# A two-layer decoder on one core: when the RMS norms' squares and mean columns are issued

## The chip, the cores and the metric

The kernel runs on one core of one Trainium2 chip. The metric is the device time of one execution in microseconds; the lower, the better. Engines are named as in the profile: PE is TensorE, ACT is ScalarE, DVE is VectorE, POOL is GpSimd, and SP's queue issues the loads.

## What is computed

The input x has 256 tokens of 1024 features, and every weight and activation is float32. Two layers are run, each as half a feed-forward step, an attention mixer, and half a feed-forward step:

```python
def rmsnorm(x, g):
    y = x * lax.rsqrt(jnp.mean(x * x, axis=-1, keepdims=True) + RMS_EPS)
    return y * g

def swiglu(h, w_gate, w_up, w_down):          # 1024 -> 2816 -> 1024
    return (jax.nn.silu(h @ w_gate) * (h @ w_up)) @ w_down

for layer in range(2):
    h = h + 0.5 * swiglu(rmsnorm(h, ffn1_norm[layer]), ...)
    hn = rmsnorm(h, mix_norm[layer])
    h = h + (mixer_a(hn, a_w_qkv, a_w_o) if layer == 0 else mixer_b(hn, b_w_q, b_w_o, *shared))
    h = h + 0.5 * swiglu(rmsnorm(h, ffn2_norm[layer]), ...)
    if layer == 0:
        shared = shared_kv(h, kv_norm, kv_w)  # keys and values for mixer_b
return rmsnorm(h, final_norm)
```

Both mixers are attention with 16 heads of 64 and rotary on 16 of the 64 features. What matters here is the norm: the factor `rsqrt(mean(x*x) + eps)` belongs to a token, so it can be applied after the products with the weights, to their result.

## The kernel before

**Precision.** Every float32 factor is split in two on the chip: a high part (`wh`, `xh`), a rounding copy on ACT, and a low part (`wl`, `xl`), the difference taken on DVE. Each product is three: high by high, high by low, low by high. In `products_t` (L198) the activations' high and low parts stand side by side, so that a weight's high part takes both in one 512-wide matmul (L203), and its low part takes the activations' high part in a 256-wide one (L206). In `product` (L189), used by the mixers, three matmuls of 512 stand in a row (L192, L194, L196).

**Order.** All instructions are written in program order; a scheduler then orders each engine's queue. `queued(p)` (L145) fixes one instruction behind another on its engine where the author wishes so, without a semaphore: whatever is issued within it stands behind the instructions that `marks[p]` holds.

**The norm.** `Norm` (L219 to L260) holds what is needed of one RMS norm. `scale` multiplies the residual stream by the gain and splits it (`x_n`: ACT L98, DVE L96). `square` squares one of the eight feature blocks on ACT (`ss_n` for the first, L237, and `sq_n` for the seven others, L240) and adds it to the running sum on POOL (L241). `finish` makes the column: four small matmuls of the sum with 1/1024 (`col_n`, PE L246), the epsilon (`v_n`, DVE L248) and the power -0.5 (`c_n`, POOL L250). `spread` makes a row of the column, for results that have features on the partitions: two diagonal matrices (`diag_n`, DVE L257), four matmuls with ones (`row_n`, PE L258) and a copy out of PSUM (`r_n`, DVE L260).

**The feed-forward opening.** `ffn_blocks` (L351) walks over the 22 blocks of 128 hidden features, two at a time. The first pair of the first layer, `f10`, is special: `opening` (L172) loads its weights in slices along the features as they arrive, splits each (`wh` at L181, `wl` at L182) and multiplies at once, feature block by feature block. `first` (L805), called per slice, loads the input, scales the blocks of this slice and squares those of the slice before. The last two squares and `norm.finish()` stand behind the loop (L410 to L413), so the column's matmuls are on PE between the opening's products and those of block 2. Block 2's gate and up products (`f_g`, `f_u`, from 1 MB loads that `unit` splits at L166 and L167) follow, then `close_all`, which spreads the row and closes the blocks before: `joined` (L332) adds an accumulator's two halves (`j_f_g`, `j_f_u`: ACT L335, DVE L336), and further steps multiply by the row. Accumulators are five PSUM buffers in a ring (`accp`), so block 3's gate product `f_g3` takes the one that block 0's gate leaves. Squares and `j_` tiles share a ring of five in SBUF (`ep`).

**The mixers.** `mixer` (L722) runs its query, key and value projections through an `Agenda`: each product of the projection advances a clock by 0.68, and calls that were put down with `agenda.after(wait, ...)` are issued once the clock reaches them. The norm's remaining steps are put down at 1.5 and on, and `norm.finish` at 8.1, in mixer a for `n1` and in mixer b for `n5` (the norm of its queries; its keys' and values' norm is finished earlier). When a projection of 128 tokens is complete, `evacuate` scales it by the column out of PSUM (`rt_a`, ACT L772), the rotary follows on DVE (L635 to L638), and `turn_in` transposes it on PE (`qt_a`, L761), put down 4.4 - 1.2 t behind it for token block t. `Pieces` (L292) splits the projection weights a few units ahead (`wh` on ACT L318, `wl` on DVE L320) and loads those behind them.

Of the kernel before, what the change touches and what calls it, by code (L numbers as in the profile page):

```python
# [12 lines left out]
AF = mybir.ActivationFunctionType  # L13
# [4 lines left out]
NT = S // P  # L18
D = 1024
KD = D // P  # L20
# [46 lines left out]
def trunk(ctx: ExitStack, tc: tile.TileContext, a: dict, out: bass.AP):  # L67
# [19 lines left out]
    def flat(ap):  # L87
        return ap.rearrange("p c n -> p (c n)")
# [83 lines left out]
    def opening(wg, wu, before):  # L172


        for k, n in OPENING:
            raw = early.get(k) or rawp.tile([P, 2, n, S], F32, tag="raw", name=f"raw_0_{k}")
            wh, wl = [wp.tile([P, 2, n, S], F32R, tag=tag, name=f"{tag}_0_{k}") for tag in ("wh", "wl")]
            before(k, n)
            for i, w in list(enumerate((wg, wu)))[k in early:]:
                nc.sync.dma_start(raw[:, i], rows(w, k, n, 0, S))  # L180
            nc.scalar.activation(wh, raw, AF.Copy)  # L181
            nc.vector.tensor_sub(wl, raw, wh.bitcast(F32))  # L182
            for j in range(n):
                yield [(wh[:, i, j, :], wl[:, i, j, :]) for i in range(2)]
# [10 lines left out]
        for ac, (wh, wl) in zip(accs, ws):  # L195
            nc.tensor.matmul(ac, xl, wh, start=False, stop=last)  # L196

    def products_t(acs, wss, xs, first, last):  # L198


        for ac, ws in zip(acs, wss):
            for i, ((wh, wl), x) in enumerate(zip(ws, xs)):
                nc.tensor.matmul(ac, wh, flat(x), start=first and i == 0, stop=False)  # L203
        for ac, ws in zip(acs, wss):
            for i, ((wh, wl), x) in enumerate(zip(ws, xs)):
                nc.tensor.matmul(ac[:, :S], wl, x[:, 0, :], start=False, stop=last and i == len(ws) - 1)  # L206
# [12 lines left out]
    class Norm:  # L219
# [23 lines left out]
        def finish(self):  # L243
            ps = trt(f"col_{self.name}")
            for t in range(NT):
                nc.tensor.matmul(ps[:, t:t + 1], self.ss[:, t * P:(t + 1) * P], mean, start=True, stop=True)  # L246
            v = sp.tile([P, NT], F32, tag="var", name=f"v_{self.name}")
            nc.vector.tensor_scalar_add(v, ps[:, :NT], EPS)  # L248
            r = sp.tile([P, NT], F32, tag="rms", name=f"c_{self.name}")
            nc.gpsimd.tensor_tensor(r, v, expo.to_broadcast([P, NT]), op=ALU.pow)  # L250
            self.col = [r[:, t:t + 1] for t in range(NT)]
# [40 lines left out]
    class Pieces:  # L292
# [1 line left out]


        def __init__(self, specs):
            self.specs, self.raws, self.parts, self.rest = specs, [], [], []

        def load(self, u):
            while len(self.raws) <= min(u, len(self.specs) - 1):  # L300
# [6 lines left out]
        def split(self, i):  # L307

            end = 2 * len(self.specs)
            while len(self.parts) <= min(i, end - 1):  # L310
                m = len(self.parts)
                u, j = divmod(m, 2)
                self.load(u + 2)
                name, k, n, _ = self.specs[u]
                k //= 2
                raw = self.raws[u][:, j * k:j * k + k]
                wh, wl = [wp.tile([P, k, n], F32R, tag=tag, name=f"{tag}_{name}_{j}") for tag in ("wh", "wl")]
                nc.scalar.activation(wh, raw, AF.Copy)  # L318
                self.parts.append([(wh[:, r, :], wl[:, r, :]) for r in range(k)])
                self.rest.append(lambda wl=wl, raw=raw, wh=wh: nc.vector.tensor_sub(wl, raw, wh.bitcast(F32)))  # L320
                while len(self.rest) > (m < end - 1):
                    self.rest.pop(0)()

        def __getitem__(self, i):
            return self.get(i)
# [25 lines left out]
    def ffn_blocks(name, wg, wu, norm, first=None, beside=(), sums=None, queue=()):  # L351

        blocks, pairs, rest = [], {}, []

        def both(f, pair):
            acs = [acc(f"{name}_{n}{f}") for n in "gu"]
            cols = slice(f % 2 * P, (f % 2 + 1) * P)
            products_t(acs, [[(wh[:, cols], wl[:, cols]) for wh, wl in w] for w in pair], norm.x, True, True)  # L360
            return acs

        def close(f, gate, up):
            g = joined(gate, f"{name}_g{f}")
            nc.vector.tensor_mul(g, g, norm.row)  # L365
            nc.scalar.activation(g, g, AF.Silu)  # L366
            u = joined(up, f"{name}_u{f}")
            nc.gpsimd.tensor_tensor(u, u, norm.row, op=ALU.mult)  # L368
            pair = f // 2
            if sums is not None and pair in sums:  # L370
                if f % 2 == 0:
                    pairs[pair] = atile([P, 2, S], name=f"act2_{name}_{f}")
                prod = pairs[pair][:, f % 2]
            else:
                prod = g
            nc.vector.tensor_mul(prod, g, u)  # L376
            x = atile([P, 2, S], F32R, name=f"act_{name}_{f}")
            parts_of(x[:, 0], x[:, 1], prod)
            while rest:
                rest.pop(0)()  # L380
            if prod is not g and f % 2:
                rest.extend(quarter_sums(pairs.pop(pair), *sums[pair], f"{name}_{f}"))
            blocks.append(x)

        done = []

        def close_all():
            if done and norm.row is None:
                norm.spread()
            for args in done:  # L390
                close(*args)
            done.clear()

        for f in range(0, KF, 2):
            if f == 0 and first is not None:
                ws = opening(wg, wu, first)
            else:
                ws = zip(*[unit(f"{name}_{n}{f}", KD, S, [(None, rows(w, 0, KD, f * P, S))], behind[:2 if f == 0 else 0])
                           for n, w, behind in (("g", wg, queue[:2]), ("u", wu, queue[2:]))])
            if f == 0:  # L400
                acs = [[(trt if i and n == "u" else acc)(f"{name}_{n}{i}") for n in "gu"] for i in range(2)]
                for k, pair in enumerate(ws):
                    for i in range(2):
                        for ac, (wh, wl) in zip(acs[i], pair):
                            cols = slice(i * P, (i + 1) * P)
                            products_t([ac], [[(wh[:, cols], wl[:, cols])]], norm.x[k:k + 1], k == 0, k == KD - 1)
                    while norm.late:
                        norm.late.pop(0)()
                if first is not None:
                    for k in range(KD - 2, KD):  # L410
                        norm.square(k)
                if norm.col is None:
                    norm.finish()  # L413
                done += [(i, *acs[i]) for i in range(2)]
                continue
            pair = list(zip(*ws))
            for call in beside[f // 2 - 1:f // 2]:
                call()
            for i in (f, f + 1):
                acs = both(i, pair)  # L420
                close_all()
                done.append((i, *acs))
        close_all()
        return blocks
# [297 lines left out]
    def mixer(name, segs, plan, wo, mask, after, queue={}):  # L722
# [15 lines left out]
        specs += [(f"{name}o_{u}", 2, D, [(None, rows(wo, 2 * u, 2, 0, D))]) for u in range(KD // 2)]  # L738
        pieces = Pieces(specs)
        agenda = Agenda()  # L740
        for norm in {id(norm): norm for norm, _, _ in segs}.values():
            for i in range(len(norm.late)):
                agenda.after(1.5 + 0.5 * i, lambda norm=norm: norm.late.pop(0)())
            if norm.col is None:
                agenda.after(8.1, norm.finish)
        scores, turn, values = attention(agenda, lambda g: (qks[g], vss.get(g)), mask, name, blocks)

        def turns(p):
# [18 lines left out]
        def evacuate(i, t, r, ac, parts):  # L767
# [16 lines left out]
                    at += n  # L784
            for g in sorted(set(turned)):
                if ("q", g, t) in heads and ("k", g, t) in heads:
                    agenda.after(4.4 - 1.2 * t if i == 0 else 3.2, turn_in, g, t)

        def projections():
            for i, (norm, x, parts) in enumerate(segs):  # L790
                acs = [acc(f"{''.join(part[0] for part in parts)}_{name}{i}_{t}") for t in range(NT)]
                for k0 in range(0, KD, 4):
                    for t in range(NT):
                        for k in range(k0, k0 + 4):
                            w = pieces[4 * i + k // 2][k % 2]
                            product([acs[t]], *x[t](k), [w], k == 0, k == KD - 1)
                            yield 0.68
                        if k0 + 4 == KD:
                            evacuate(i, t, norm.col[t], acs[t], parts)

        agenda.run(projections())
        agenda.run(out_t(f"{name}o", pieces, base, blocks, after, queue))
# [2 lines left out]
    def first(k, n):  # L805
        cols = slice(GX + k * S if k else 0, GX + (k + n) * S)
        nc.sync.dma_start(both[:, cols], a["gains_xT"][:, cols])
        for i in range(k, k + n):
            n0.scale(i)
        for i in range(k - 2, k - 2 + n):  # L810
            if i >= 0:
                n0.square(i)

    n0, n1, n2 = Norm(0, "n0"), Norm(1, "n1"), Norm(2, "n2")
    n3, n5, n6 = Norm(4, "n3"), Norm(5, "n5"), Norm(6, "n6")
# [108 lines left out]
```

## Time and profile before

| | before |
|---|---|
| median of 3 runs | 980.28 us (980.27 to 980.37) |
| the profiled execution | 980.13 us |
| its span, first to last instruction | 978.4 us |
| granted TensorE clock | 0.998 |
| PE busy | 967.5 us, 99% |
| DVE busy | 813.0 us, 83% |
| ACT busy | 612.7 us, 63% |
| POOL busy | 287.0 us, 29% |
| HBM | 176 MB moved, 180 GB/s in the mean |

A row of the timeline gives the start in microseconds from the span's start, the duration, the engine, the line, the operation, what it writes from what it reads, a count where equal instructions follow each other, and in brackets the engine's idle time before it and what ended that. Buffer numbers are left out of names, so `wl_f_g` is the low part of any gate weight. A PE row's duration includes the time that a product takes to drain; how close two products follow is read from their starts.

### The profile page before, as it was taken

The page shows a single profiled execution, that of the slowest core. Times are in us where ns is not written, and L with a number is a line of the kernel's source. Part 1 is how long each engine was busy: PE and PEld are TensorE (multiplying, and loading weights), DVE is VectorE, ACT ScalarE, POOL GpSimd, SP SyncE. Part 2 cuts the span into 40 slices and gives each one's busy share as a digit, 9 for nine tenths or more (in the row PEclk, how much of TensorE's full clock was granted, in tenths as well). Part 3 has the DMA queues.
Part 4 walks back from the last instruction along what each step waited for, and adds up shares of the span by engine and source line. Part 5 has one row for each costly group of instructions (what it writes and reads, how often), then busy time and mean ns, then how long its engine had stood idle before and what let it go on. Part 6 is the DMA issues. An engine that isn't in the chain of part 4 may idle for free.

```text
span 978.4 us, 14860 instructions
## 1 busy us (share of the span) xinstructions
PE 967.5 (99%) x5391; PEld 831.9 (85%) x5391; DVE 813.0 (83%) x1383; ACT 612.7 (63%) x1131; POOL 287.0 (29%) x242
## 2 busy tenths in 40 slices
PE   8999999999999999999999999999999999999997
PEld 6888888878889888888888888888888998888886
DVE  7988899887878788889898888987787878888995
ACT  7655657567777665556576655655677756666561
POOL 3211246132332211146032121612142322112461
PEclk9999999999999999999999999999999999999999
DMA  9875536664334556546755556483734345564341
GB/s 317 259 238 187 197 133 216 219 212 157 133 98 152 180 186 189 184 153 208 256 172 173 172 177 212 169 277 114 249 131 136 116 145 172 186 202 173 130 172 43
DMA packets 126857, 176.00 MB, mean 180 GB/s; under 512 B 3392, under 2 KB 106304, under 8 KB 126784
## 3 DMA queue, kind: packets, MB, share of 16 engines
q1 hardware_dynamic: 125936, 174.01, 53.7%
q10 hardware_dynamic: 848, 1.05, 0.3%
q8 instruction: 42, 0.69, 0.3%
q14 instruction: 31, 0.25, 0.1%
HBM read 173.99 MB, written 1.05 MB: 179 GB/s over the span
## 4 chain that ended last, share of the span: by engine, by line
PE 92%; DVE 4%; ACT 2%; issue 1%; POOL 1%; DMA 0%; SPq 0%; POOLq 0%; DVEq 0%; ACTq 0%
PE f_g L203 16%; PE f_u L203 16%; PE f_u L206 8%; PE f_g L206 8%; PE dn_f_d L196 6%; PE dn_f_d L192 6%; PE dn_f_d L194 6%; PE dn_f_d_m L196 1%; PE dn_f_d_m L194 1%; PE dn_f_d_m L192 1%; PE qk_a L192 1%; PE qk_a L196 1%; PE qk_a L194 1%; DVE x_n L96 1%; PE q_b L192 1%
## 5 line engine op out<-in xcount | busy, mean ns | idle before, releaser
L368 POOL TENSOR_TENSOR j_f_u<-j_f_u,r_n 128x256 f32<-128x256 f32 x88 | 92.3, 1051 | 360.8 <-DVE j_f_u L336 338.0
L203 PE MATMUL f_g<-x_n,wh_f_g 128*128 128x512 f32 x688 | 180.5, 394 | 0.0
L203 PE MATMUL f_u<-x_n,wh_f_u 128*128 128x512 f32 x688 | 177.2, 390 | 0.0
L203 PEld LDWEIGHTS f_u<-x_n,wh_f_u 128*128 128x128 f32 x688 | 129.2, 188 | 27.3
L203 PEld LDWEIGHTS f_g<-x_n,wh_f_g 128*128 128x128 f32 x688 | 124.0, 189 | 22.7
L167 DVE TENSOR_TENSOR wl_f_u<-raw_f_u,wh_f_u 128x1024 fp32r<-128x1024 f32 x86 | 113.1, 1316 | 1.1 <-ACT wh_f_u L166 1.0
L167 DVE TENSOR_TENSOR wl_f_g<-raw_f_g,wh_f_g 128x1024 fp32r<-128x1024 f32 x86 | 104.3, 1230 | 2.8 <-ACT wh_f_g L166 2.8
L206 PE MATMUL f_u<-x_n,wl_f_u 128*128 128x256 f32 x688 | 103.3, 283 | 0.0
L206 PE MATMUL f_g<-x_n,wl_f_g 128*128 128x256 f32 x688 | 102.7, 282 | 0.0
L206 PEld LDWEIGHTS f_g<-x_n,wl_f_g 128*128 128x128 f32 x688 | 96.4, 190 | 6.3
L166 ACT ACTIVATE wh_f_u<-raw_f_u 128x1024 fp32r<-128x1024 f32 x86 | 88.0, 1049 | 12.0 <-PE f_g L203 7.5
L166 ACT ACTIVATE wh_f_g<-raw_f_g 128x1024 fp32r<-128x1024 f32 x86 | 89.6, 1049 | 4.7 <-PE f_g L203 2.8
L206 PEld LDWEIGHTS f_u<-x_n,wl_f_u 128*128 128x128 f32 x688 | 91.6, 192 | 0.0
L366 ACT ACTIVATE j_f_g<-j_f_g 128x256 f32<-128x256 f32 x88 | 36.7, 417 | 87.2 <-DVE j_f_g L365 86.9
L241 POOL TENSOR_TENSOR ss_n<-ss_n,sq_n 128x256 f32<-128x256 f32 x42 | 38.4, 913 | 148.8 <-ACT sq_n L240 146.8
L98 ACT ACTIVATE act_f<-j_f_g 128x256 fp32r<-128x256 f32 x58 | 23.9, 418 | 56.4 <-DVE j_f_g L376 56.4
L376 DVE TENSOR_TENSOR j_f_g<-j_f_g,j_f_u 128x256 f32<-128x256 f32 x58 | 27.9, 487 | 30.1 <-POOL j_f_u L368 30.1
L484 POOL TENSOR_TENSOR sum_f_d_6b<-sum_f_d_6ac,raw_f_d 128x512 f32<-128x512 f32 x4 | 45.5, 11371 | 17.6 <-DVE sum_f_d_6ac L483 13.2
L336 DVE TENSOR_TENSOR j_f_g<-f_g,j_f_g 128x256 f32<-128x256 f32 x88 | 36.6, 416 | 11.9 <-ACT j_f_g L335 11.9
L677 POOL TENSOR_SCALAR sm_b<-sm_b,ls_b 128x128 f32<-128x128 f32 (+1 forms) x32 | 28.5, 907 | 55.7 <-DVE ls_b L675 29.6
L335 ACT ACTIVATE j_f_u<-f_u 128x256 f32<-128x256 f32 x88 | 33.0, 375 | 15.0 <-PE row_n L258 14.0
L365 DVE TENSOR_TENSOR j_f_g<-j_f_g,r_n 128x256 f32<-128x256 f32 x88 | 41.4, 474 | 0.7
(565 smaller groups left out, 2369.3 us busy)
## 6 DMA issues: line engine op xcount, KB each, us to landing
raw_f_d<-in_ffn_w_down_dram SPq DMA_DIRECT2D x44, 1024.0 KB, 4.9
raw_f_g<-in_ffn_w_gate_dram SPq DMA_DIRECT2D x43, 1024.0 KB, 5.2
raw_f_u<-in_ffn_w_up_dram SPq DMA_DIRECT2D x43, 1024.0 KB, 5.2
raw_qka<-in_a_w_qkv_dram SPq DMA_DIRECT2D x16, 512.0 KB, 4.7
raw_va<-in_a_w_qkv_dram SPq DMA_DIRECT2D x4, 1024.0 KB, 5.4
raw_ao<-in_a_w_o_dram SPq DMA_DIRECT2D x4, 1024.0 KB, 4.9
raw_kvb<-in_kv_w_dram SPq DMA_DIRECT2D x8, 512.0 KB, 4.7
raw_qb<-in_b_w_q_dram SPq DMA_DIRECT2D x4, 1024.0 KB, 5.9
```

Of the source, the lines that this page charges most:

```text
L166: nc.scalar.activation(wh, r, AF.Copy)
L167: nc.vector.tensor_sub(wl, r, wh.bitcast(F32))
L192: nc.tensor.matmul(ac, xh, wh, start=first, stop=False)
L194: nc.tensor.matmul(ac, xh, wl, start=False, stop=False)
L196: nc.tensor.matmul(ac, xl, wh, start=False, stop=last)
L203: nc.tensor.matmul(ac, wh, flat(x), start=first and i == 0, stop=False)
L206: nc.tensor.matmul(ac[:, :S], wl, x[:, 0, :], start=False, stop=last and i == len(ws) - 1)
L241: nc.gpsimd.tensor_tensor(self.ss, self.ss, sq, op=ALU.add)
L365: nc.vector.tensor_mul(g, g, norm.row)
L366: nc.scalar.activation(g, g, AF.Silu)
L368: nc.gpsimd.tensor_tensor(u, u, norm.row, op=ALU.mult)
L484: nc.gpsimd.tensor_tensor(b[:, 0], ac[:, 0], raw[:, 3], op=ALU.add)
```

## The change

Three things move; the operations and their numbers stay as they are.

1. In the opening of `f10` all eight squares are issued behind the loop, and on ACT behind the last split of the opening's weights (`marks["opening"]`). Their adds on POOL follow them.
2. `norm.finish` of this norm is no longer called behind the opening but inside block 2's `products_t`, behind the eight wide products of its gate. The instructions on each engine stand as follows by this: on PE the column comes behind those eight and ahead of the eight wide up products; on DVE `v_n` stands behind the four `wl` subtractions of block 2, the two `diag_n`, one subtraction of block 4 and `r_n` follow, and the first `j_f_g` comes behind `r_n`, where it stood ahead of the row before. Other feed-forward steps finish their norm as before.
3. In the mixers the column is put down at 8.7 for the first norm (mixer a) and at 14.0 for the other (mixer b); the subtractions of `Pieces` that come later are queued behind `v_n` on DVE; the evacuation of a projection goes through the agenda too, 0.6 later while the column is missing; and `turn_in` comes 4.4 - 0.8 t behind. The attention's steps, which are put down from there, come about one product later against PE's queue. The loads of the rotary table, the masks and the final gain each go one step earlier among the weight loads.

```diff
         def opening / for k, n in OPENING:
-            nc.scalar.activation(wh, raw, AF.Copy)
+            marks["opening"] = [nc.scalar.activation(wh, raw, AF.Copy)]
             nc.vector.tensor_sub(wl, raw, wh.bitcast(F32))
...
-    def products_t(acs, wss, xs, first, last):
+    def products_t(acs, wss, xs, first, last, between=None):
         for ac, ws in zip(acs, wss):
             for i, ((wh, wl), x) in enumerate(zip(ws, xs)):
                 nc.tensor.matmul(ac, wh, flat(x), start=first and i == 0, stop=False)
+            if between is not None:
+                between()
+                between = None
...
-            nc.vector.tensor_scalar_add(v, ps[:, :NT], EPS)
+            marks[self.name] = [nc.vector.tensor_scalar_add(v, ps[:, :NT], EPS)]
...
-            self.specs, self.raws, self.parts, self.rest = specs, [], [], []
+            self.specs, self.raws, self.parts, self.rest, self.behind = specs, [], [], [], None
...
-                while len(self.rest) > (m < end - 1):
-                    self.rest.pop(0)()
+                with queued(self.behind):
+                    while len(self.rest) > (m < end - 1):
+                        self.rest.pop(0)()
...
-            products_t(acs, [[...] for w in pair], norm.x, True, True)
+            products_t(acs, [[...] for w in pair], norm.x, True, True,
+                       norm.finish if norm.col is None else None)
...
                 if first is not None:
-                    for k in range(KD - 2, KD):
-                        norm.square(k)
-                if norm.col is None:
+                    with queued("opening"):
+                        for k in range(KD):
+                            norm.square(k)
+                elif norm.col is None:
                     norm.finish()
...
+        def column(norm):
+            norm.finish()
+            pieces.behind = norm.name
+
             if norm.col is None:
-                agenda.after(8.1, norm.finish)
+                agenda.after(8.7 if norm is segs[0][0] else 14.0, column, norm)
...
-                    agenda.after(4.4 - 1.2 * t if i == 0 else 3.2, turn_in, g, t)
+                    agenda.after(4.4 - 0.8 * t if i == 0 else 3.2, turn_in, g, t)
...
                         if k0 + 4 == KD:
-                            evacuate(i, t, norm.col[t], acs[t], parts)
+                            agenda.after(0.6 if norm.col is None else 0.0,
+                                         lambda t=t, i=i, norm=norm, ac=acs[t], parts=parts:
+                                         evacuate(i, t, norm.col[t], ac, parts))
...
         def first:
         for i in range(k, k + n):
             n0.scale(i)
-        for i in range(k - 2, k - 2 + n):
-            if i >= 0:
-                n0.square(i)
```

More of the change, by code (lines that the diff above doesn't have):

```diff
@@ L359, in both @@
             cols = slice(f % 2 * P, (f % 2 + 1) * P)
-            products_t(acs, [[(wh[:, cols], wl[:, cols]) for wh, wl in w] for w in pair], norm.x, True, True)
+            products_t(acs, [[(wh[:, cols], wl[:, cols]) for wh, wl in w] for w in pair], norm.x, True, True,
+                       norm.finish if norm.col is None else None)
             return acs
```

## The prediction

> **What bounds the kernel now.** I read the page's engine table first, then the chain that ended last, then TensorE's list of waits, and only then the timeline around each wait.
>
> ```profile
> span 978.4 us, 14860 instructions
> PE 967.5 (99%) x5391; PEld 831.9 (85%) x5391; DVE 813.0 (83%) x1383; ACT 612.7 (63%) x1131; POOL 287.0 (29%) x242
> PE f_g L206 <- DVE wl L182: 0.8, 1, 0.8
> PE f_g L203 <- ACT wh L181: 0.8, 2, 0.5
> PE col_n L246 <- POOL ss_n L241: 0.6, 1, 0.6
> PE qt_a L761 <- ACT wh_qka L318: 0.2, 1, 0.2
> PE qt_a L761 <- DVE rt_a L638: 0.2, 1, 0.2
> ```
>
> TensorE is busy for 967.5 of 978.4 us, so a change that leaves its products alone can only win back gaps between them. The last five rows are all of its listed waits but the warm-up's, and the change aims at each of them. All are under a microsecond: 2.6 us in sum, with further tenths around them that "busy" hides, because a product that waits for a late operand inside its pipeline is shown as running. I therefore read starts, not idle columns: a 512-wide product is followed by the next start 0.23 us later, a 256-wide one 0.12.
>
> **Opening, TensorE's side.** These are TensorE's rows, then ScalarE's, VectorE's and GpSimd's.
>
> ```profile
> 9.63 0.50 PE L203 MATMUL f_g<-x_n,wh 128*128 128x512 f32 x1 [0.46 <-ACT wh L181]
> 16.08 0.39 PE L203 MATMUL f_g<-x_n,wh 128*128 128x512 f32 x1
> 17.28 0.38 PE L206 MATMUL f_g<-x_n,wl 128*128 128x256 f32 x1 [0.81 <-DVE wl L182]
> 19.93 0.50 PE L246 MATMUL col_n<-mean,ss_n 128*128 128x1 f32 x4
> 20.29 2.10 PE L203 MATMUL f_g<-x_n,wh_f_g 128*128 128x512 f32 x8
> 22.23 1.98 PE L203 MATMUL f_u<-x_n,wh_f_u 128*128 128x512 f32 x8
> 25.96 0.60 PE L258 MATMUL row_n<-diag_n,ones 128*128 128x128 f32 x4
> 26.32 0.94 PE L203 MATMUL f_g<-x_n,wh_f_g 128*128 128x512 f32 x3
> ```
> ```profile
> 12.64 0.71 ACT L240 ACTIVATE sq_n<-gains_hT 128x256 f32<-128x256 f32 x2
> 13.26 1.04 ACT L181 ACTIVATE wh<-raw 128x1024 fp32r<-128x1024 f32 x1
> 15.66 2.01 ACT L166 ACTIVATE wh_f_g<-raw_f_g 128x1024 fp32r<-128x1024 f32 x2 [0.75 <-DMA raw_f_g<-in_ffn_w_gate_dram]
> 18.67 2.01 ACT L166 ACTIVATE wh_f_u<-raw_f_u 128x1024 fp32r<-128x1024 f32 x2 [1.01 <-DMA raw_f_u<-in_ffn_w_up_dram]
> ```
> ```profile
> 9.61 1.23 DVE L182 TENSOR_TENSOR wl<-raw,wh 128x1024 fp32r<-128x1024 f32 x1 [0.90 <-ACT wh L181]
> 15.47 1.75 DVE L182 TENSOR_TENSOR wl<-raw,wh 128x1024 fp32r<-128x1024 f32 x1
> 17.15 2.89 DVE L167 TENSOR_TENSOR wl_f_g<-raw_f_g,wh_f_g 128x1024 fp32r<-128x1024 f32 x2
> 20.47 0.16 DVE L248 TENSOR_SCALAR v_n<-col_n 128x2 f32<-128x2 f32 x1 [0.43 <-PE col_n L246]
> 21.46 0.48 DVE L257 TENSOR_SCALAR diag_n<-ident,c_n 128x128 f32<-128x128 f32 x2 [0.83 <-POOL c_n L250]
> 21.86 2.35 DVE L167 TENSOR_TENSOR wl_f_u<-raw_f_u,wh_f_u 128x1024 fp32r<-128x1024 f32 x2
> 24.13 0.42 DVE L336 TENSOR_TENSOR j_f_g<-f_g,j_f_g 128x256 f32<-128x256 f32 x1
> ```
> ```profile
> 8.71 0.74 POOL L241 TENSOR_TENSOR ss_n<-ss_n,sq_n 128x256 f32<-128x256 f32 x1 [7.42 <-ACT sq_n L240]
> 13.18 4.64 POOL L241 TENSOR_TENSOR ss_n<-ss_n,sq_n 128x256 f32<-128x256 f32 x4 [0.47 <-ACT sq_n L240]
> L368 POOL TENSOR_TENSOR j_f_u<-j_f_u,r_n 128x256 f32<-128x256 f32 x88 | 92.3, 1051 | 360.8 <-DVE j_f_u L336 338.0
> ```
>
> Before, six of the eight squares stand on ScalarE between the casts (`wh`), at 0.31 us each, and their adds on GpSimd run beside VectorE's subtractions. The cost is on both: the last `wl` takes 1.75 us where one with GpSimd idle took 1.23, and it starts late. Behind the last `wh` the squares cost the opening nothing. The loads still bind: two 1 MB weight loads ended ScalarE's waits at 15.66 and 18.67, 3.0 us apart, so the load ahead of them landed near 12.65, and `wh` can go from 13.26 to 12.65, no earlier. It ends at 13.69, its `wl` near 15.0 instead of 17.22. The step of 1.20 us from 16.08 to 17.28 then shrinks to 0.23 (0.97 won); the 0.46 before 9.63 goes too, since `wh` there stands behind two squares (0.61); two smaller late operands make about 0.45. Together 1.9 us: the opening's products end near 18.05 instead of 19.93.
>
> **Opening, what is late next.** The column needs all seven adds. The squares now run from 13.7; the first add from 14.4. An add alone took 0.74, four beside VectorE took 4.64, or 1.16 each. So the sum is complete between 14.4 + 7 x 0.74 = 19.6 and 14.4 + 7 x 1.16 = 22.5. VectorE is idle from about 15 to 17.3 in the new order: one add at 1.16, two at 0.74, four at 1.05 (the mean of 88 GpSimd products beside VectorE) give 21.2. TensorE gets to the column after f_g2's eight wide products, at 18.05 + 1.9 = 19.95, and stands still in front of it for 1.2 us (0 to 2.5). Everything queued behind the column on TensorE waits along: f_u2's products. From the column to f_g3 TensorE has 0.36 + (26.32 - 22.23) = 4.45 us of work, so f_g3 could start at 25.65.
>
> But f_g3 writes the accumulator that f_g0 leaves, and VectorE's add `j_f_g` frees it. Before, that add was done at 24.55, ahead of the row. In the new order it stands behind four subtractions, `v_n`, the two `diag`, one more subtraction and `r_n`, the copy of the row. Four subtractions from 17.5 at 2.89 + 2.35 us end near 22.7; `v_n` to `diag` took 0.99, so `diag` comes at 23.75; the next subtraction (1.18) ends at 25.4; the row, which TensorE reaches at 25.3, is there at 25.65; `r_n`, of the size of `j_f_g`, and `j_f_g` itself at 0.4 each and a step of 0.1 bring f_g3 to about 26.5. Earliest (second f_u cast at 20.68 + 1.2, then the same steps, no wait for the row) it is 25.3; latest (sum at 22.5) 27.6. Against 26.32: 1.0 gained to 1.3 lost, and I take **0.15 lost**. What is won in the opening is given back before the third product column.
>
> The rows show each engine slowed beside the other, adds 0.74 to 1.16 and subtractions 1.23 to 1.75. The Trainium skill, page "SBUF — State Buffer", section "Who interferes with whom", says that VectorE with two SBUF inputs and a GpSimd operation that reads SBUF hold an exclusive lock in turn: the loser stands still for a whole instruction. By it, adds and subtractions would alternate; that result is the last rival below.
>
> **Mixer a.** Its rows, with mixer b's column last.
>
> ```profile
> 199.44 0.50 PE L196 MATMUL qk_a<-wh_qka,x_n 128*128 128x512 f32 x1
> 200.04 0.61 PE L246 MATMUL col_n<-mean,ss_n 128*128 128x1 f32 x4
> 205.76 0.63 PE L761 MATMUL qt_a<-ident,rt_a 128*128 128x128 f32 x4 [0.23 <-ACT wh_qka L318]
> 207.95 0.63 PE L761 MATMUL qt_a<-ident,rt_a 128*128 128x128 f32 x4 [0.18 <-DVE rt_a L638]
> 199.31 1.75 DVE L320 TENSOR_TENSOR wl_va<-raw_va,wh_va 128x1024 fp32r<-128x1024 f32 x1
> 202.12 0.15 DVE L248 TENSOR_SCALAR v_n<-col_n 128x2 f32<-128x2 f32 x1
> 202.35 1.62 POOL L250 TENSOR_TENSOR c_n<-v_n,expo 128x2 f32<-128x2 f32 x1 [2.37 <-DVE v_n L248]
> 204.01 0.69 ACT L772 ACTIVATE rt_a<-qk_a,c_n 128x512 f32<-128x512 f32 x1 [4.58 <-POOL c_n L250]
> 682.41 0.61 PE L246 MATMUL col_n<-mean,ss_n 128*128 128x1 f32 x4 [0.57 <-POOL ss_n L241]
> ```
>
> The column starts 0.60 after the product at 199.44, where 0.23 is the step: 0.37 lost. One product (0.68) later it finds the sum. `v_n`, which stood behind two subtractions until 202.12, stands ahead of them, so it runs at about 200.9 and GpSimd's power (1.62 here) ends near 202.7 instead of 203.97. The held subtraction of `wl_va` (199.31) now starts at 201; its products come behind the first `qt_a` (205.76), so nobody waits. `rt_a` on ScalarE then starts 1.2 us earlier, while `turn_in` comes 0.68 later: both `qt_a` waits, 0.39 and 0.35 by their starts, should go; I leave 0.1 for the first, since its rotation now meets two subtractions. Mixer a: 0.37 + 0.64 = **1.0 us**.
>
> **Mixer b.** The column (682.41) waits 0.57, 0.73 by its starts, and moves some eight products back, where the sum is long done. `c_n` of this norm is needed only when q's products end, behind those. **0.73 us.**
>
> **What lies behind both mixers.** Evacuation one product later shifts the attention chain by 0.68 against TensorE's queue. At mixer a's end that slack can be read:
>
> ```profile
> 299.00 0.42 DVE L94 TENSOR_TENSOR oT_a<-o_a,oT_a 128x256 fp32r<-128x256 f32 x1 [0.48 <-ACT oT_a L98]
> 300.61 0.28 PE L602 MATMUL ot_ao<-oT_a,wh_ao 128*128 128x256 f32 x1
> ```
>
> `oT_a`'s low half is done at 299.42 and read near 300.6: 1.1 us, of which 0.7 are spent. No wait, priced 0 (if the cover fails, the price per mixer is up to 0.7). The squares, the column and the loads of masks keep their counts; those loads go one step earlier among weight loads of 3.0 us each that are far ahead by then, 0.
>
> **Sum.** -0.15 + 1.0 + 0.73 = 1.6 us. The profiled execution took 980.13, so 978.55; the median of the runs is 0.15 above it, so the forecast is 978.7. About 0.2%, 1.96 us, is what a measurement of this kernel tells from no change, and the forecast lies just inside it.
>
> **Rivals.**
> - *As forecast*: the mixers' waits go, the opening gives nothing or little back either way (+0.5 to -0.6). 978.0 to 979.3. Chance 0.47.
> - *The opening keeps its gain*: GpSimd's adds run at 0.74 since VectorE is idle in front of them, and the chain to f_g3 takes its earliest value, 1.0, or even only TensorE's work, 24.4, for 1.9. For it: the 0.74 at 8.71. Against: four subtractions in a row stand beside the last adds. 976.6 to 977.9; chance 0.22.
> - *Gains in the mixers come back as waits*: columns' 0.37 and 0.73 are won, but later transposes or the end of the chains stall by 0.7 in each mixer, or the transposes' 0.74 stay. 979.2 to 980.4; chance 0.20. It also covers a change that does less than it says, because loads set the opening.
> - *Slower: adds and subtractions by turns.* From 17.3 the last four adds each stand behind a whole subtraction: 4 x (1.23 + 0.74) = 7.9, sum at 25.2; TensorE stands still 5 us in front of the column, the row is reached at 29.3 and f_g3 starts near 30.4, 4.1 late. Less 1.75 from the mixers: 2.3 slower, 982.6. It turns the sign once the sum is later than about 22.9, and passes 0.2% at 24.8. Against it: four adds took 4.64 beside a busy VectorE, not 7.9, and the 88 products average 1.05. Chance 0.11. By the page's rule it should be this case; the rows agree with a milder one.
>
> Faster by over 0.2% are the second case and a third of the first, 0.38; slower the last and a few hundredths of the third, 0.14; the rest 0.48. The range of 8 in 10 runs from 976.9, inside the second case, to 980.6, past the third, and leaves out the last.
>
> **What would show it.** In the new profile: no `wl L182` wait in TensorE's list, opening products ending near 18; a new wait of `col_n` on `ss_n` at about 20 of some 1.2 us, the seven adds ending near 21; f_g3 at 26.5, released by `j_f_g` on VectorE; no waits at `qt_a` or at mixer b's column. I'm wrong if f_g3 starts before 25.5 or after 27, or if new rows with `oT_a`, `po_a` or `qt_a` stand in the list.

## The result, and the profile after

| | before | changed |
|---|---|---|
| median | 980.29 us (980.25 to 980.67, 6 runs) | 984.85 us (983.42 to 986.29, 6 runs) |
| ratio to before | | 1.0044, 95% interval 1.0031 to 1.0057 |
| profiled execution | 980.13 us, span 978.4 | 983.59 us, span 981.8 |

The change makes the kernel 4.6 us slower, and the time lies 4.2 us above the range. Its runs also lie 2.9 us apart, where those of before lie within 0.4 here and within 1.4 in the largest later set, of 31 runs. TensorE's waits in the profile after, in us in all, times, and the longest:

```profile
PE col_n L249 <- POOL ss_n L244: 3.1, 1, 3.1
PE f_g L203 <- DVE j_f_g L340: 0.8, 1, 0.8
PE ot_bo L608 <- ACT oT_b L98: 0.4, 1, 0.4
PE pt_b L688 <- DVE nm_b L670: 0.3, 1, 0.3
PE po_a L707 <- DVE pT_a L693: 0.2, 1, 0.2
```

Every wait that the change aimed at is gone from the list, and five others stand in their place. The first is the opening's. Its timeline on TensorE:

```profile
17.86 2.06 PE L203 MATMUL f_g<-x_n,wh_f_g 128*128 128x512 f32 x8
23.01 0.60 PE L249 MATMUL col_n<-mean,ss_n 128*128 128x1 f32 x4 [3.10 <-POOL ss_n L244]
23.68 3.39 PE L203 MATMUL f_u<-x_n,wh_f_u 128*128 128x512 f32 x8
28.88 0.60 PE L261 MATMUL row_n<-diag_n,ones 128*128 128x128 f32 x4
30.34 1.88 PE L203 MATMUL f_g<-x_n,wh_f_g 128*128 128x512 f32 x7 [0.85 <-DVE j_f_g L340]
```

The opening's own products end 2.07 us earlier, as meant: the next block starts at 17.86 where the column stood at 19.93. Then TensorE stands in front of the column for 3.1 us, f_u's eight wide products take 3.2 us from first start to the next group (1.8 before), and f_g3 starts at 30.34 for 26.32, 4.02 late. The sum is late on GpSimd. Behind the row of all seven adds, the rows come from three narrow windows of the timeline (a row counts all equal instructions that reach into its window, so the starts are what to read), with VectorE's below:

```profile
14.34 8.62 POOL L244 TENSOR_TENSOR ss_n<-ss_n,sq_n 128x256 f32<-128x256 f32 x7 [13.05 <-ACT sq_n L243]
18.03 3.26 POOL L244 TENSOR_TENSOR ss_n<-ss_n,sq_n 128x256 f32<-128x256 f32 x2
19.71 3.25 POOL L244 TENSOR_TENSOR ss_n<-ss_n,sq_n 128x256 f32<-128x256 f32 x2
21.37 1.59 POOL L244 TENSOR_TENSOR ss_n<-ss_n,sq_n 128x256 f32<-128x256 f32 x1
17.75 1.28 DVE L167 TENSOR_TENSOR wl_f_g<-raw_f_g,wh_f_g 128x1024 fp32r<-128x1024 f32 x1 [2.85 <-ACT wh_f_g L166]
18.96 1.76 DVE L167 TENSOR_TENSOR wl_f_g<-raw_f_g,wh_f_g 128x1024 fp32r<-128x1024 f32 x1
20.64 1.74 DVE L167 TENSOR_TENSOR wl_f_u<-raw_f_u,wh_f_u 128x1024 fp32r<-128x1024 f32 x1
```

Four adds are through by 18.03, and the last three start 1.68 and 1.66 us apart, each between two starts of a subtraction, which have the same steps from 18.96 on (20.64, then 22.30). The two engines go by turns, an add and a 1024-wide subtraction to a period. The granted clock by the microsecond (stretch, length, busy time of PE, PEld, DVE, ACT and POOL with counts, then the clock and DMA):

```profile
22.00:23.00 1.00, 0.00 (x0) 0.00 (x0) 1.00 (x2) 1.00 (x3) 0.96 (x1) 1.00 1.10 347
23.00:24.00 1.00, 0.99 (x7) 0.94 (x8) 1.00 (x2) 1.00 (x3) 0.00 (x0) 0.97 1.10 348
24.00:25.00 1.00, 1.00 (x4) 0.81 (x3) 0.17 (x3) 0.48 (x1) 0.71 (x1) 0.50 1.10 349
25.00:26.00 1.00, 1.00 (x3) 0.73 (x3) 1.00 (x3) 0.00 (x0) 0.00 (x0) 0.50 1.10 348
26.00:27.00 1.00, 1.00 (x4) 0.79 (x3) 0.56 (x1) 0.00 (x0) 0.00 (x0) 0.50 1.13 352
27.00:28.00 1.00, 1.00 (x9) 1.00 (x8) 0.00 (x0) 0.00 (x0) 0.00 (x0) 0.83 1.06 346
```

TensorE ran at half clock for 3.4 us (0.03 + 0.50 x 3 + 0.17 lost, doubled), just after the wait; that is 1.7 us of work that it didn't do. So the 4.02 are: -2.07 for the opening's products, +3.3 from the end of f_g2's wide products (eight steps of 0.23 behind 17.86, near 19.7) to the column, +1.7 for the clock, +1.1 at f_g3 (1.46 from row to f_g3, where it was 0.36): 4.0.

Subtracting the starts of equal products in the two traces gives the mixers' part. After the opening the changed kernel is 4.02 late; the column and the first transposes of mixer a bring that to 2.93, and its further course back to 3.35, which holds for all products up to mixer b. Mixer b's column brings it to 2.53, and its end back to 3.44. Won 1.09 + 0.82, given back 0.42 + 0.91.

### The profile page after: what moved, and what is told of

Read it like the earlier page. It is cut to its first block, busy times and chain, and to the rows that moved or that the text cites. A ratio compares the mean times of both kernels' runs of the same rounds, so it can differ in the third digit from the quotient of the medians.

```text
span 981.8 us, 14861 instructions
## 1 busy us (share of the span) xinstructions
PE 968.8 (99%) x5391; PEld 833.4 (85%) x5391; DVE 812.4 (83%) x1383; ACT 612.0 (62%) x1131; POOL 290.9 (30%) x242
## 3 DMA queue, kind: packets, MB, share of 16 engines
q10 hardware_dynamic: 848, 1.05, 0.3%
HBM read 173.99 MB, written 1.05 MB: 178 GB/s over the span
## 4 chain that ended last, share of the span: by engine, by line
PE 93%; DVE 2%; ACT 2%; DMA 1%; POOL 1%; issue 1%; ACTq 0%; POOLq 0%; SPq 0%; DVEq 0%
PE f_u L203 16%; PE f_g L203 16%; PE f_u L209 8%; PE f_g L209 8%; PE dn_f_d L196 6%; PE dn_f_d L194 6%; PE dn_f_d L192 6%; PE dn_f_d_m L196 1%; PE dn_f_d_m L194 1%; PE dn_f_d_m L192 1%; PE qk_a L192 1%; PE qk_a L196 1%; PE qk_a L194 1%; PE v_a L192 1%; PE q_b L192 1%; PE kv_b L192 1%
## 5 line engine op out<-in xcount | busy, mean ns | idle before, releaser
L490 POOL TENSOR_TENSOR sum_f_d_6b<-sum_f_d_6ac,raw_f_d 128x512 f32<-128x512 f32 x4 | 42.6, 10656 | 17.6 <-DVE sum_f_d_6ac L489 13.2
L683 POOL TENSOR_SCALAR sm_a<-sm_a,ls_a 128x128 f32<-128x128 f32 (+1 forms) x32 | 30.3, 962 | 47.9 <-DVE ls_a L681 42.2
```

The lines of the kernel that those rows point to most:

```text
L490: nc.gpsimd.tensor_tensor(b[:, 0], ac[:, 0], raw[:, 3], op=ALU.add)
L683: nc.gpsimd.tensor_scalar(sm[:, seg], sm[:, seg], ls[:, t:t + 1], None, op0=ALU.mult)
```

## The experiments

**The two parts alone.** e1_opening undoes the third part of the change, e2_mixers the first two.

```diff
 e1_opening, against the changed kernel
-                agenda.after(8.7 if norm is segs[0][0] else 14.0, column, norm)
+                agenda.after(8.1, norm.finish)
-                    agenda.after(4.4 - 0.8 * t if i == 0 else 3.2, turn_in, g, t)
+                    agenda.after(4.4 - 1.2 * t if i == 0 else 3.2, turn_in, g, t)
-                            agenda.after(0.6 if norm.col is None else 0.0, lambda ...: evacuate(...))
+                            evacuate(i, t, norm.col[t], acs[t], parts)
 e2_mixers, against the changed kernel
-                    with queued("opening"):
-                        for k in range(KD):
-                            norm.square(k)
-                elif norm.col is None:
+                    for k in range(KD - 2, KD):
+                        norm.square(k)
+                if norm.col is None:
+        (in first) for i in range(k - 2, k - 2 + n):
+            if i >= 0:
+                n0.square(i)
```

> Only the opening's part of the change; the mixers' columns, evacuations and transposes stand as before. Theory A (the loss is the opening's: the adds on GpSimd take turns with VectorE's subtractions, so the column waits 3.1 us and f_g3 starts 4.0 us late): 980.28 + 4.0 = 984.3, and at least 983.5. Theory B (the loss comes from the attention chain, one product later, and the opening's late start is caught up further on): 980 to 981.

> Only the mixers' part of the change; squares and column of the opening as before. Theory A: starts of TensorE's products in the two traces say that both mixers together won about 1.9 us at their columns and transposes and gave back about 1.3, so 979.7. Theory B: 982 or more.

e1_opening took 984.98 us (983.93 to 985.83; ratio 1.0046, 1.0031 to 1.0061), e2_mixers 979.76 (979.60 to 980.00; ratio 0.9993, 0.9983 to 1.0003). The loss is the opening's. The mixers alone win 0.6 us of 980.38, which by the interval can't be told from nothing. The profiled execution of e1_opening took 985.77 us and its f_g3 was 5.7 us late, not 4.0, with 2.9 us of wait at this column. Its clock says where the rest is:

```profile
23.00:24.00 1.00, 0.81 (x4) 0.81 (x5) 1.00 (x1) 1.00 (x4) 0.14 (x1) 0.56 1.09 346
24.00:25.00 1.00, 1.00 (x4) 0.90 (x5) 0.38 (x2) 0.66 (x1) 0.52 (x1) 0.50 1.12 354
28.00:29.00 1.00, 1.00 (x7) 1.00 (x6) 0.00 (x0) 0.00 (x0) 0.00 (x0) 0.50 1.06 337
29.00:30.00 1.00, 1.00 (x7) 1.00 (x7) 0.00 (x0) 0.00 (x0) 0.00 (x0) 0.53 0.39 129
30.00:31.00 1.00, 1.00 (x10) 0.98 (x9) 0.00 (x0) 0.02 (x1) 0.00 (x0) 1.00 0.07 25
```

The stretches from 25 to 28 read 0.50 too. Half clock for 6.8 us (0.44 + 5 x 0.50 + 0.47 lost, doubled), twice the 3.4 of the other execution.

**Is it the standing still that lowers the clock?** e3_warm adds matmuls that compute nothing ahead of the column.

```diff
             ps = trt(f"col_{self.name}")
+            for _ in range(13 if self.name == "n0" else 0):
+                nc.tensor.matmul(ps, fill[:, :P], fill, start=True, stop=True)
```

> The changed kernel, with 13 matmuls that nobody needs, 512 wide like those at the start, ahead of the opening's column, into its own PSUM bank. They fill the 3.1 us in which TensorE stood still (13 x 0.23 = 3.0 us). Theory A with the clock (the granted clock fell to 0.50 from 24 to 27 us because TensorE stood still): the clock stays at 1.00, f_u's eight wide products take 1.9 us where they took 3.2, f_g3 starts near 28.8 and the time is 1.5 us below the changed kernel's. Rival (the slow products wait for operands, and the clock's fall has another cause): f_u's products stay at 3.2 us and the time is the changed kernel's.

It took 981.11 us (980.78 to 981.92), 3.7 below the changed kernel's median. The adds are as late as there, the column starts at 23.34, and the clock stays at 1.00 in every stretch from 18 to 30 us:

```profile
20.07 2.55 PE L249 MATMUL col_n<-fill 128*128 128x512 bf16 x11
23.34 0.61 PE L251 MATMUL col_n<-mean,ss_n 128*128 128x1 f32 x4 [0.72 <-POOL ss_n L244]
23.81 2.09 PE L203 MATMUL f_u<-x_n,wh_f_u 128*128 128x512 f32 x8
28.01 2.09 PE L203 MATMUL f_g<-x_n,wh_f_g 128*128 128x512 f32 x8
```
```profile
20.00:22.00 2.00, 2.00 (x10) 0.90 (x10) 2.00 (x2) 1.44 (x2) 1.89 (x2) 1.00 1.11 349
22.00:24.00 2.00, 1.28 (x8) 0.76 (x7) 2.00 (x2) 1.46 (x2) 1.29 (x1) 1.00 1.10 351
24.00:26.00 2.00, 2.00 (x11) 1.66 (x11) 1.17 (x5) 1.40 (x5) 0.71 (x1) 1.00 1.09 346
```

Two of the 13 added matmuls ran earlier, at 10.32 and 10.55, between the opening's products; the other eleven cut TensorE's wait from 3.10 to 0.72. So the clock is the standing still's. It won more than the expected 1.5 for two reasons: the median of the changed kernel lies 1.26 above its profiled execution, and in this order the first `j_f_g` adds stand ahead of `r_n`, so that f_g3 follows the row at once and not 1.1 later. The spread fell to 1.1 us from 2.9.

**Is it the turns?** e6_held gives GpSimd's adds no neighbour: block 2's four subtractions are issued behind `v_n`.

```diff
-                nc.vector.tensor_sub(wl, r, wh.bitcast(F32))
+                held.append(lambda: nc.vector.tensor_sub(wl, r, wh.bitcast(F32)))   # f10, block 2
...
+        def column():
+            norm.finish()
+            with queued(norm.name):
+                while held:
+                    held.pop(0)()
```

> The changed kernel, with block 2's four subtractions on VectorE held back until v_n, so that GpSimd's adds have no company. Theory A (an add takes 0.75 us alone and about 1.6 to 1.9 beside 1024-wide subtractions): the first add beside the opening's last subtraction 1.2, six at 0.75, sum complete near 20.3 and not 23, a wait of 0.2 to 0.4 at the column, no fall of the clock. The held subtractions then make f_g3 late by another way: near 27.9, 1.6 behind the kernel before; with the mixers' -0.6, 981.3. Rival (the adds are slow at this place whatever VectorE does): seven adds still take 8.6 us, 983 or more.

981.22 us (980.73 to 982.56). Seven adds, without company but for the first:

```profile
13.76 6.08 POOL L247 TENSOR_TENSOR ss_n<-ss_n,sq_n 128x256 f32<-128x256 f32 x7 [12.46 <-ACT sq_n L246]
19.89 0.61 PE L252 MATMUL col_n<-mean,ss_n 128*128 128x1 f32 x4
20.77 1.64 POOL L256 TENSOR_TENSOR c_n<-v_n,expo 128x2 f32<-128x2 f32 x1 [0.94 <-DVE v_n L254]
27.49 2.11 PE L206 MATMUL f_g<-x_n,wh_f_g 128*128 128x512 f32 x8 [1.01 <-DVE j_f_g L343]
```

2.5 us less for the same adds, 0.3 of wait in front of the column by the starts (the eight wide products begin at 17.74) where it was 3.3, clock 1.00 from 20 to 28 us, and, as expected, the held subtractions make f_g3 late in another way. The power `c_n`, of two elements a row, now meets a subtraction and takes 1.64 us; in the changed kernel, with VectorE idle, it took 0.71 (at 24.19). The price is thus the neighbour's, not the operation's.

**Can the adds go elsewhere?** e4_vector_adds puts the seven adds on VectorE, which is idle there.

```diff
-                nc.gpsimd.tensor_tensor(self.ss, self.ss, sq, op=ALU.add)
+                add = nc.vector if self.name == "n0" else nc.gpsimd
+                add.tensor_tensor(self.ss, self.ss, sq, op=ALU.add)
```

> The changed kernel, with the opening's seven adds on VectorE in place of GpSimd; they fall into its idle time from 14.9 to 17.7 us. Theory A (the turns between GpSimd and VectorE make the sum late): sum complete near 17, no wait at the column, no fall of the clock, f_g3 near 25.6 for 26.32 before, and with the mixers as in the changed kernel 979.0. Rival (the sum is late because the squares come late on ScalarE, whichever engine adds): the column still waits over 1 us and the time stays above 981.

979.42 us (979.00 to 980.46; ratio 0.9991, 0.9982 to 1.0001):

```profile
14.91 3.07 DVE L245 TENSOR_TENSOR ss_n<-ss_n,sq_n 128x256 f32<-128x256 f32 x6
19.03 0.42 DVE L245 TENSOR_TENSOR ss_n<-ss_n,sq_n 128x256 f32<-128x256 f32 x1
19.87 0.50 PE L250 MATMUL col_n<-mean,ss_n 128*128 128x1 f32 x4
24.19 0.68 PE L262 MATMUL row_n<-diag_n,ones 128*128 128x128 f32 x4
26.09 2.12 PE L203 MATMUL f_g<-x_n,wh_f_g 128*128 128x512 f32 x8 [1.22 <-DVE j_f_g L341]
```

No wait at the column. The last add went behind a subtraction, to 19.45, still in time. What is left is the wait for `j_f_g`, 1.2 us: f_g3 is only 0.23 earlier than before. TensorE stands idle in that wait, from 24.87 to 26.09, and the clock stays at 1.00 in every stretch from 18 to 30 us.

**Does the column's place cost anything by itself?** e7_between leaves the squares and mixers as before and only calls `finish` inside block 2's products. Against the kernel before:

```diff
-            products_t(acs, [[...] for w in pair], norm.x, True, True)
+            products_t(acs, [[...] for w in pair], norm.x, True, True,
+                       norm.finish if norm.col is None else None)
...
-                if norm.col is None:
+                elif norm.col is None:
                     norm.finish()
```

> Only the column inside block 2's products; the squares and their adds stand between the slices as in the kernel before, and the mixers as before. Theory A (moving the squares makes the loss, not the column's place): the sum is complete at 17.8, TensorE meets no wait at the column, f_g3 starts within 0.5 us of 26.3, time 980.3 within 0.4. Rival (the column's place makes the loss, since v_n stands behind four subtractions): 981.3 or more.

980.49 us (980.07 to 980.86; ratio 1.0003, 0.9993 to 1.0012): nothing. In that order two `j_f_g` and `j_f_u` adds stand ahead of `r_n`, and f_g3 follows the row by 0.36 as in the kernel before.

**What comes behind the adds.** e9_early_joins is e4_vector_adds with the joining adds of the first three accumulators issued ahead of `spread`; `close` takes them as `ready` in place of its own.

```diff
             if done and norm.row is None:
+                if first is not None:
+                    ready = {0: [joined(ac, f"{name}_{n}0") for n, ac in zip("gu", done[0][1:])],
+                             1: [joined(done[1][1], f"{name}_g1")]}
                 norm.spread()
             for args in done:
-                close(*args)
+                close(*args, ready.get(args[0], ()))
```

> e4_vector_adds, and the joining adds of the opening's first three accumulators are issued ahead of the row, so that f_g3's accumulator is free before the row is made. Theory A (in e4_vector_adds f_g3 at 26.1 waited 1.2 us for j_f_g alone): f_g3 starts near 24.4, 1.9 earlier than in the kernel before, and the time is 977.8. Rival (the next one in line binds, the row or the subtractions of block 2): f_g3 not before 25.5, 979.

977.99 us (977.66 to 978.60; ratio 0.9978, 0.9968 to 0.9987). The first product of f_g3 starts at 24.09, 2.2 earlier than before, even ahead of the row; the row now stands within f_g3, and TensorE's products behind it come 1.7 earlier:

```profile
24.09 0.39 PE L203 MATMUL f_g<-x_n,wh_f_g 128*128 128x512 f32 x1
24.41 0.71 PE L262 MATMUL row_n<-diag_n,ones 128*128 128x128 f32 x4
```

**The mixers' rest.** e5_direct is e2_mixers, but only the projection that must wait for its column is evacuated through the agenda.

```diff
-                            agenda.after(0.6 if norm.col is None else 0.0, lambda ...: evacuate(...))
+                            if norm.col is None:
+                                agenda.after(0.6, lambda ...: evacuate(...))
+                            else:
+                                evacuate(i, t, norm.col[t], acs[t], parts)
```

> The mixers' part of the change alone (as e2_mixers), but a projection whose norm's column is there already is evacuated at once, as in the kernel before; only the first one of mixer a, which waits for the column, goes through the agenda. Theory A (what the mixers give back, 0.4 us in mixer a and 0.9 in mixer b, comes from the attention chain standing one product later): mixer b gives nothing back, mixer a still its 0.4 for the first heads, so 980.3 - 1.9 + 0.4 = 978.8. Rival (it comes from the subtractions held behind v_n or from the later transposes): as e2_mixers, 979.8.

978.40 us (977.94 to 979.39; ratio 0.9981, 0.9971 to 0.9990), 1.36 below e2_mixers. TensorE's list there has no wait but the opening's:

```profile
PE busy L118 <- DVE fill L115: 1.4, 1, 1.4
PE f_g L203 <- ACT wh L181: 1.2, 2, 0.7
PE f_g L209 <- DVE wl L182: 0.8, 1, 0.8
```

`ot_bo`, `pt_b` and `po_a`, which e2_mixers and the changed kernel share, are gone. By the starts it won 1.18 in mixer a and 0.86 in mixer b and gave nothing back. `agenda.after(0.0, ...)` was the cause: a call put down so is issued only after the next product, and so every projection, also those whose column had long been there, was evacuated a product later. The 0.4 that I left for mixer a's first heads weren't lost either.

**All three.** e10_all is e9_early_joins with e5_direct's evacuation.

> The three mends together: adds on VectorE, the joining adds ahead of the row (e9_early_joins) and evacuation at once where the column is there (e5_direct). Theory A (opening and mixers add up): 977.99 less what e5_direct was below e2_mixers, 979.76 - 978.40 = 1.36: 976.6. Rival (a later stage takes part of it back): 977.3 or more.

977.56 us over five runs, but those were 976.25, 976.36, 977.56, 977.75 and 978.04; in the profiled one, of 977.75, a product of the opening waits 0.53 at 9.76 us for a cast behind its load, and f_g3 starts 0.84 later than in e9_early_joins (24.93 for 24.09). Its loads came later: the last split of the opening starts at 13.78 behind its load, in e9_early_joins at 12.65. So both were run beside each other once more, with the changed kernel:

> e9_early_joins once more, on the chip of the next run, so that the two can be set against each other. If what e10_all lost against its forecast came with that chip's loads (its first products began later in that execution), this kernel stays at 978.0 beside it.

> e10_all once more, beside e11_joins_again. Theory A (opening and mixers add up): 1.2 to 1.4 below e11_joins_again on the same chip. Rival (a later stage takes part back): at most 0.6 below it.

> The changed kernel once more, for a second profile. Its runs lay between 983.4 and 986.3. Theory A with the clock (the half clock lasts longer in some executions): the time over what the first profiled execution took, 983.59, stands in f_u's, f_g's and the following products at a granted clock of 0.50, while the column's wait is 3.1 us as before. Rival (the wait itself varies): the clock's stretch is the same 3.3 us, the wait another.

e11_joins_again took 977.92 us (977.50 to 978.98), e12_all_again 976.28 (976.18 to 976.44; ratio to before 0.9957, 0.9943 to 0.9970), 1.6 below, a little more than expected: the parts add up. This version beats both kernels there, by 4.1 and 8.3 us; e10_all, the same kernel on another chip, was 2.7 below the kernel before (ratio 0.9965, 0.9952 to 0.9979). That late loads lengthened three of its five runs is seen in the profiled one alone. e13_changed_again took 984.60 (983.33 to 985.41). Its profiled execution took 984.07, 0.48 more than the first; neither of the two theories held: the half clock again lasted 3.4 us, the column's wait 3.11, and the 0.48 came with the column's start, 23.47 for 23.01, as the loads had come later. That the half clock can double is shown by e1_opening's profile alone. That it makes the rest of the spread of 2.9 us fits the mean clocks (0.997 in the runs of 983.42 and 983.59, 0.996 in those from 984.66 to 986.29) but wasn't seen in a trace of those runs.

## Why the prediction was wrong

- *The opening's products 1.9 us earlier*: right, 2.07.
- *The sum complete at 21.2 and a wait of 1.2 us*: wrong, and the step that carries the miss. I priced the last four adds at 1.05, the mean of 88 products. The three beside 1024-wide subtractions took 1.6 each, at a step of 1.68; the sum was complete at 22.96 and the wait 3.1. A single row that I quoted, `c_n` at 1.62 beside a wide subtraction, had the right price. The group of four adds in 4.64 us hid it: the first met the end of a wide subtraction, the second and third the short ones of `x_n` (the third started ahead of the next wide one, which then took 1.75), and the last, which started within that wide one, took twice as long as either. It is this row of a narrow window in the kernel before, behind adds of 1.20, 0.80 and 0.80:

```profile
16.22 1.61 POOL L241 TENSOR_TENSOR ss_n<-ss_n,sq_n 128x256 f32<-128x256 f32 x1
```

  I had named the turns as the slower rival and gave it 0.11; its forecast for f_g3, 30.4, came out at 30.34, partly by accident: its sum at 25.2 was 2.2 too late, and the clock's 1.7, which it hadn't, made up for most of that. The Trainium skill, page "SBUF — State Buffer", sections "SBUF: two separate sides" and "Who interferes with whom", had the mechanism, an exclusive lock held for a whole instruction. The starts that interlock at 1.68 us agree with it in kind; the period is below the 1.97 of an add and a subtraction in full as the profile has their durations.
- *Nothing for the clock*: missing from the sum altogether, 1.7 us or more. I put a wait on TensorE at its own length and no more. The Trainium skill, page "TensorE: Matmul & The Clock Gate", section "Part 1: The HAM clock gate", says that an idle window of about 3.4 us halves the clock and that windows run freely. Here less sufficed: 3.10 and 3.11 us of wait in the two profiled executions of the changed kernel, 2.94 in e1_opening. The half clock lasted 3.4 us in the first two and 6.8 in e1_opening, one or two such windows. Waits of 0.72 in e3_warm and 1.22 in e4_vector_adds left the clock alone; between 1.22 and 2.94 no run shows it.
- *f_g3 bound by `j_f_g` behind the row*: right in kind; the sum had 0.85 for it (26.5 for 25.65), and by the starts it took 1.1 us in the changed kernel and 1.5 in e4_vector_adds (26.09 less 24.19 and the 0.36 of before). The latest case, 27.6, is 27.8 by the same steps from a sum at 22.5, which decides nothing.
- *Mixers -1.73*: right at the columns and transposes, -1.91 by the starts. *Slack behind the mixers, priced 0*: wrong, 0.42 + 0.91 given back. I read it at the end of mixer a alone; mixer b's is smaller (waits at `pt_b` and `ot_bo`).

Of the whole miss, 984.85 against 978.7, 3.9 us are the opening's in the profiled execution (+4.02 for +0.15) and 1.15 the mixers' (-0.58 for -1.73); 1.1 is the distance of the median from the profiled execution, 1.26 where before it was 0.15.

## What to carry to other kernels

Price an operation by the one row that had the same neighbour, not by a group's mean: one GpSimd add here took 0.74 us by itself and 1.6 beside a wide subtraction. Before work is taken off the start of a stage, look at what it will meet where it is put: spread over the loads the squares and their sum cost the opening some 2 us, and gathered at the end the sum stood on the path for 3.3 and took the clock with it, until an engine that was idle there (VectorE) did it at 0.4 to 0.5 an add. And a wait on TensorE of some 3 us cost more than itself here: the half clock behind it took a further 1.7 us, or twice that. If it can't be avoided, matmuls that nobody needs can hold the clock, as in e3_warm.

## What was not expected of the hardware

The half clock came at the wait's end or after it, not with its beginning. In the changed kernel TensorE resumed at 23.01 and the granted clock was still 0.97 in the microsecond from 23, then 0.50 until 27.3; in e13_changed_again it resumed at 23.47, and the microsecond from 24 shows 0.62, the first below 1.00; in e1_opening it resumed at 23.19, and the microsecond from 23 shows 0.56. So a profile shows the cost in products that have nothing to wait for, in a row that only looks long (eight in 3.39 us), and the list of waits doesn't hold it.
